# The second MLP layer of a diffusion block on one core: one more level of the seven-product scheme

## The chip, the cores and the metric

The kernel runs on one core of a Trainium2 chip. A core has a matrix engine (TensorE, PE in the profile) that reads SBUF and writes PSUM, a vector engine (VectorE, DVE), a scalar engine (ScalarE, ACT), a general engine (GpSimd, POOL) and a queue engine that starts transfers (SyncE, SP). Each takes its instructions in the order of the program; semaphores order the engines among each other. The metric is the device time of one launch in microseconds, median of 3 runs: 2862.96 (2862.67 to 2863.17).

## The reference

One layer is computed for 256 context tokens and 2048 latent tokens of width 1024: modulated norm, input projection, attention and Fourier mixing, output projection with a gated residual, and then an MLP with a squared ReLU. The part that matters here is the last:

```
def sq_relu_mlp(h, w1, w2):
    return jnp.square(jax.nn.relu(h @ w1)) @ w2
...
        xs = xs + g2 * sq_relu_mlp(h, w1[l], w2[l])
```

The second product has 2304 tokens (18 tiles of 128), an inner width of 4096 and 1024 output columns. All of it is in 32-bit floats.

## The kernel before

**Precision.** Every operand of a large product is split into a high part, which ScalarE makes by a copy to the type F32R, and a low part, which VectorE makes by subtracting the high part from the operand (two inputs in SBUF). `mm3` (line 93) then issues three matmuls for one product of tiles: high x high, high x low, low x high. TensorE reads F32R in one pass.

**Seven products.** The MLP's second layer is cut in two along tokens (9 tiles each), inner width (16 tiles of 128 each) and output columns (512 each), and the four block products per quadrant are replaced by the seven products of Strassen's scheme in Winograd's form. `PO` (line 1383) is their order: 1, 2, 6, 7, 5, 3, 4. The sums of token blocks are made in the first layer by GpSimd (`g_add`, line 1784) and stored to DRAM (`sop`, tile `sd`); the sums of weight blocks were made earlier too (`tsum`); product 4 subtracts two of its raw weight tiles at the time of use.

**The second layer's loop** (from line 2020) runs over the 7 products `i`, over 3 blocks `b` of 3 token tiles, and over 16 inner tiles `k`. For each `k` it issues 3 x 3 matmuls: the stationary operand is a token tile (128 x 128), the moving one is a weight tile of 512 columns. Three PSUM banks collect a block; six are in use in turn. `t_prep` (line 1401) splits one weight tile of 512 columns, 16 per product; `s_prep` (line 1415) splits token operands in pieces of 768 columns, 24 per product. `t_load` and `s_load` bring the raw operands in by SP's queue some steps ahead. When a block is done, `y_post` (line 1973) combines its three banks with the running sums `UU` and `U3` in SBUF, and, in the products 2, 5, 3 and 4, which finish outputs, multiplies by the gate, adds the residual and lets `y_store` store it. GpSimd has no instruction in this loop. The split operands live in rings: `op` (9 pairs of 512 columns, shared with the first layer) and a second ring of 13.

The order of the work is the order of the Python calls, written out by hand (`tc.manual_schedule()`): each engine runs its own instructions in that order, as soon as the semaphores allow.

Of the kernel before, what the change touches and what calls it, by code (L numbers as in the profile page):

```python
# [37 lines left out]
def f32(ap):  # L38
    return ap.bitcast(F32)


def body(tc, a, out):
    nc = tc.nc
    ctx = ExitStack()
    with ctx:
# [1336 lines left out]
        OPB, AHEAD = 9, 6  # L1382
        PO = (1, 2, 6, 7, 5, 3, 4)
        w2s = a["w2"][0].rearrange("(n k p) o -> p n k o", p=P, k=16)
        TR, TO, SR, SO, own = {}, {}, {}, {}, {}

        def op(nm, shared=True):
            if shared:
                return [ms2.tile([P, 512], F32R, tag=f"op{x}", name=f"op{x}{nm}", bufs=OPB) for x in "hl"]
            return [own["wk"].tile([P, 512], F32R, tag=f"t{x}", name=f"t{x}{nm}", bufs=16 + AHEAD - OPB) for x in "hl"]  # L1390

        def t_load(n):

            p, k = PO[n // 16], n % 16
            TR[n] = []
            for rc in {1: (11,), 2: (21,), 3: (22,), 5: (0,), 7: (1,), 6: (2,), 4: (2, 21)}[p]:
                r, c = divmod(rc, 10)
                src = w2s[:, r - 1, k, (c - 1) * 512:c * 512] if r else tsum[k][:, c]
                TR[n].append(raw(f"b{rc}_{n}", src))

        def t_prep(n):
            src, *more = TR.pop(n)
            for t in more:
                nc.vector.tensor_sub(src, src, t)
            hi, lo = op(f"T{n}", n % (16 + AHEAD) < OPB)
            nc.scalar.copy(hi, src)
            nc.vector.tensor_sub(lo, src, f32(hi))
            TO[n] = hi, lo

        def s_load(m):  # L1410
            i, r = divmod(m, 12)
            b, c = divmod(r, 4)
            SR[m] = hr_load(f"sr{m}", sop[PO[i]][b][:, 4 * c:4 * c + 4, :])

        def s_prep(m):
            src = SR[m // 2][:, m % 2 * 2:m % 2 * 2 + 2, :]
            pool, bufs = (ms2s, 2) if m % 3 < 2 else (own["t6"], 1)
            hi, lo = (pool.tile([P, 2, 384], F32R, tag=f"s{x}", name=f"s{x}{m}", bufs=bufs) for x in "hl")
            nc.scalar.copy(hi, src)  # L1419
            nc.vector.tensor_sub(lo, src, f32(hi))  # L1420
            SO[m] = hi, lo

# [280 lines left out]
        with c5r, ExitStack() as c5:  # L1706
# [157 lines left out]
            with tc.manual_schedule():  # L1864
                for n, (q, p) in enumerate(ITEMS):
# [70 lines left out]
                    if q == NQ - 1 and p == 7:  # L1936
                        s_load(0)
                        for n in range(4):
                            t_load(n)
                        s_load(1)  # L1940
# [191 lines left out]
```

## Time and profile before

| what | us |
|---|---|
| median of 3 runs | 2862.96 |
| the profiled execution, first to last instruction | 2861.4 |
| stage 0 to 530 (conditioning, projections), TensorE busy | 516.31 |
| stage 530 to 1245 (attention), TensorE busy | 707.81 |
| stage 1245 to 1470 (output projection), TensorE busy | 223.17 |
| stage 1470 to 2170 (MLP, first layer), TensorE busy | 698.45 |
| stage 2170 to 2857 (MLP, second layer), TensorE busy | 685.91 |

The profile was taken on one execution; its span lies 1.6 us below the median of the runs. How to read its lines: a group of instructions is named by line, engine and operation, output tile <- input tiles, shapes and count, then busy time, mean duration in ns, and the idle time of the engine before them with what ended it. A line of a timeline has start and duration in us. A line of the windows has, for a stretch, the busy time and number of instructions of PE, PEld (weight loads), DVE, ACT and POOL, then the granted clock of TensorE, the share of the transfer engines and GB/s. In the second layer the weight tiles of the split operands are called `thT`, `tlT`, `ophT`, `oplT`, and the token pieces `sh` and `sl`.

### The profile page before, as it was taken

The page shows a single profiled execution, that of the slowest core. Times are in us where ns is not written, and L with a number is a line of the kernel's source. Part 1 is how long each engine was busy: PE and PEld are TensorE (multiplying, and loading weights), DVE is VectorE, ACT ScalarE, POOL GpSimd, SP SyncE. Part 2 cuts the span into 40 slices and gives each one's busy share as a digit, 9 for nine tenths or more (in the row PEclk, how much of TensorE's full clock was granted, in tenths as well). Part 3 has the DMA queues.
Part 4 walks back from the last instruction along what each step waited for, and adds up shares of the span by engine and source line. Part 5 has one row for each costly group of instructions (what it writes and reads, how often), then busy time and mean ns, then how long its engine had stood idle before and what let it go on. Part 6 is the DMA issues. An engine that isn't in the chain of part 4 may idle for free.

```text
span 2861.4 us, 43224 instructions
## 1 busy us (share of the span) xinstructions
PE 2831.7 (99%) x15109; PEld 2455.9 (86%) x15109; DVE 2018.0 (71%) x3393; ACT 1548.2 (54%) x3505; POOL 1073.3 (38%) x890
## 2 busy tenths in 40 slices
PE   8999999999999999999999999999999999999999
PEld 5888888688888888888889999999998888888887
DVE  7767886898988989864477777778775354345554
ACT  4333323798989989853356565556555332333221
POOL 1211223798999989942223333333332000000000
PEclk9999999999999999999999999999999999999999
DMA  7776777421211212036767676667747464445663
GB/s 284 219 207 198 230 213 237 172 106 38 73 71 53 106 38 99 23 124 201 242 221 232 223 246 228 221 219 238 234 167 255 147 202 135 138 144 185 206 206 111
DMA packets 392780, 492.94 MB, mean 172 GB/s; under 512 B 26467, under 2 KB 306384, under 8 KB 389490
## 3 DMA queue, kind: packets, MB, share of 16 engines
q1 hardware_dynamic: 387136, 479.73, 50.9%
q0 software_dynamic: 1872, 7.28, 0.8%
q10 hardware_dynamic: 3554, 3.17, 0.4%
q8 instruction: 119, 1.95, 0.3%
q14 instruction: 99, 0.81, 0.1%
HBM read 312.58 MB, written 179.59 MB: 172 GB/s over the span
## 4 chain that ended last, share of the span: by engine, by line
PE 54%; DVE 1%; DMA 0%; ACT 0%; issue 0%; SPq 0%; POOL 0%; DVEq 0%; POOLq 0%
PE ps L94 8%; PE ps L95 8%; PE ps L96 8%; PE pB L1749 2%; PE pB L1747 2%; PE pB L1748 2%; PE pA L1748 2%; PE pC L1748 2%; PE pA L1749 2%; PE pC L1747 2%; PE pA L1747 2%; PE pC L1749 2%; PE po L94 2%; PE po L96 2%; PE po L95 2%; PE pD L1749 1%
## 5 line engine op out<-in xcount | busy, mean ns | idle before, releaser
L1085 DVE TENSOR_REDUCE mxs<-Ss 128x1 f32<-128x512 f32 x636 | 405.4, 686 | 65.5 <-PE Ss L1080 55.1
L1420 DVE TENSOR_TENSOR sl<-sr,sh 128x768 fp32r<-128x768 f32 x168 | 161.8, 964 | 331.5 <-ACT sh L1419 331.1
L1120 POOL TENSOR_TENSOR P0s<-P0s,P1s 128x1024 f32<-128x1024 f32 (+2 forms) x128 | 378.6, 2958 | 10.7
L1419 ACT CAST sh<-sr 128x768 fp32r<-128x768 f32 x168 | 140.6, 838 | 418.3 <-PE ps L95 418.3
L1789 POOL TENSOR_TENSOR gs<-g,g 128x384 f32<-128x384 f32 x48 | 69.7, 1452 | 468.5 <-ACT g L1759 418.9
L1104 ACT ACTIVATE P1s<-Ss,mxs 128x512 f32<-128x512 f32 x318 | 215.4, 694 | 36.3 <-DVE mxs L1088 35.3
L94 PE MATMUL pj<-wh,hh 128*128 128x512 f32 x576 | 228.8, 397 | 2.0 <-DVE hh L555 2.0
L94 PE MATMUL ps<-thT,sh 128*128 128x512 f32 x585 | 227.6, 389 | 0.0
L95 PE MATMUL ps<-tlT,sh 128*128 128x512 f32 x585 | 227.6, 389 | 0.0
L96 PE MATMUL ps<-thT,sl 128*128 128x512 f32 x585 | 227.6, 389 | 0.0
L95 PE MATMUL pj<-wl,hh 128*128 128x512 f32 x576 | 227.1, 394 | 0.5 <-DVE wl L516 0.5
L96 PE MATMUL pj<-wh,hl 128*128 128x512 f32 x576 | 225.6, 392 | 0.0
L1104 ACT ACTIVATE P0s<-Ss,mxs 128x512 f32<-128x512 f32 x318 | 214.3, 691 | 5.6 <-DVE mxs L1088 5.0
L1135 PE MATMUL pts<-ident,P0s 128*128 128x128 f32 x1280 | 191.7, 273 | 4.5 <-DVE als L1147 1.8
L1080 PE MATMUL Ss<-KS0s,Qs 128*128 128x512 f32 x636 | 190.1, 419 | 0.4 <-ACT P1s L1104 0.4
L1080 PE MATMUL Ss<-KS1s,Qs 128*128 128x512 f32 x636 | 188.7, 420 | 1.5 <-ACT P0s L1104 1.4
L1758 ACT ACTIVATE g<-uz 128x384 f32<-128x384 f32 x144 | 75.7, 526 | 200.2 <-DVE uz L1781 174.1
L1135 PEld LDWEIGHTS pts<-ident,P0s 128*128 128x128 f32 x1280 | 151.3, 140 | 35.9 <-issue 4.8
L1119 POOL TENSOR_SCALAR P1s<-P1s,tots 128x1024 f32<-128x1024 f32 (+2 forms) x128 | 171.9, 1343 | 5.8
L1147 DVE TENSOR_TENSOR als<-pts,ahs 128x512 fp32r<-128x512 f32 x256 | 165.9, 681 | 6.9 <-ACT ahs L1142 6.7
L94 PE MATMUL ps<-ophT,sh 128*128 128x512 f32 x423 | 164.7, 389 | 1.1 <-DVE uz L1781 1.1
L96 PE MATMUL ps<-ophT,sl 128*128 128x512 f32 x423 | 164.6, 389 | 0.0
(536 smaller groups left out, 8073.9 us busy)
## 6 DMA issues: line engine op xcount, KB each, us to landing
sr<-sd SPq DMA_DIRECT2D x84, 768.0 KB, 4.5
a<-in_w SPq DMA_DIRECT2D x184, 256.0 KB, 4.2
sd<-gs SPq DMA_DIRECT2D x192, 192.0 KB, 1.9
sd<-g SPq DMA_DIRECT2D x144, 192.0 KB, 2.1
wm<-in_w_mod SPq DMA_DIRECT2D x32, 512.0 KB, 5.2
Qs<-qd SPq DMA_DIRECT2D x32, 512.0 KB, 4.0
b<-in_w SPq DMA_DIRECT2D x64, 256.0 KB, 5.8
b<-tsum SPq DMA_DIRECT2D x64, 256.0 KB, 4.7
```

The costliest lines, as they stand in the source:

```text
L94: nc.tensor.matmul(ps, lh, rh, start=first, stop=False)
L95: nc.tensor.matmul(ps, lh, rl, start=False, stop=False)
L96: nc.tensor.matmul(ps, ll, rh, start=False, stop=last)
L1080: nc.tensor.matmul(S[:, :w], self.Q[:, x, m, j * P:j * P + P], self.hd.KS[m][:, b * 512:b * 512 + w], start=(x == 0), stop=(x == 1))
L1085: nc.vector.tensor_reduce(self.mx[j][:, m, b:b + 1], self.S[j, m, b], axis=AX.X, op=ALU.max)
L1104: nc.scalar.activation(dst, S, AF.Exp, bias=self.mx[j][:, m, 6:7], accum_out=self.sm[j][:, m, b:b + 1])
L1119: nc.gpsimd.tensor_scalar(p, p, tot[:, 3:4], 0.0, op0=ALU.mult, op1=ALU.add)
L1120: nc.gpsimd.tensor_add(d, d, p)
L1135: nc.tensor.transpose(pt[:, c:c + P], self.p0[j][:, (kb + t) * P:(kb + t + 1) * P], ident)
L1747: nc.tensor.matmul(ps, wh[:, c], hh[:, k, :], start=first and k == 0, stop=False, skip_group_check=True)
L1748: nc.tensor.matmul(ps, wh[:, c], hl[:, k, :], start=False, stop=False, skip_group_check=True)
L1749: nc.tensor.matmul(ps, wl[:, c], hh[:, k, :], start=False, stop=k == 3, skip_group_check=True)
```

## The change

Each of the seven products, until now a plain product of (9 token tiles) x (16 inner tiles) x 512 columns, is itself done by the same seven-product scheme: 8 of the token tiles are cut in two halves of 4, the inner tiles in two halves of 8, and the columns in two halves of 256. The ninth token tile ("o") is done plainly, with 512 columns. A product is now 56 units `u`: 7 parts `s` of 8 inner tiles `k`. A unit issues 4 x 3 matmuls of 256 columns, and in the parts 0 and 2 another 3 of 512 columns for the ninth tile. The 4 tiles of a part share one PSUM tile of 1024 columns (two banks); three of these and two of one bank are in use in turn.

The sums of operands that the inner scheme needs are made in SBUF, in place, by GpSimd: `y_sum` on weight tiles, 256 columns each, 4 x 8 per product; `x_sum` on token rows, 3 x 4 of 1024 columns and 8 of 512 per product. Afterwards `prep` splits the operands for each unit as before (ScalarE copy, VectorE subtraction), 3 units ahead. The results are put together by `s_copy` and `t7_copy` (ScalarE), `u3_make` (VectorE and GpSimd), `pre` (GpSimd, 1024 columns) and `fin` (VectorE, one input in PSUM). `gain` and `resid` are VectorE's multiplication by the gate and addition of the residual, 1024 columns each.

Weight tiles wait in `ya` (8 tiles, tag `raw`) and `yb` (8), token rows in `hr` and `x3`, `x20`, `x21` and a ring of 5 (`x12`); most are loaded again for the next product once their last use in this one is over. The half row that `x12` holds is loaded twice per product. `do(u, ...)` files a task under the unit at which it is issued; tasks of rank under 2 come ahead of that unit's `prep`, the others behind it.

The core of the diff (`-` lines of the loop that it replaces, described above, are left out):

```diff
@@ -1379,49 +1379,114 @@
-        OPB, AHEAD = 9, 6
+        OPB = 9
...
+        UPS, LSP = 56, 3
+        TA, TB, B1, B2, B4, X12, PT, PS_ = {}, {}, {}, {}, {}, {}, {}, {}
...
+        def t_load(i, k):
+            src, *more = t_src(i, k)
+            if k < 8:
+                t = TA[i, k] = raw(f"ya{i}_{k}", src)
+            else:
+                t = TB[i, k - 8] = own["wk"].tile([P, 512], F32, tag="yb", name=f"yb{i}_{k}", bufs=8)
+                nc.sync.dma_start(t, src)
+            for m in more:
+                d = own["wk"].tile([P, 512], F32, tag="yt", name=f"yt{i}_{k}", bufs=2)
+                nc.sync.dma_start(d, m)
+                nc.vector.tensor_sub(t, t, d)
...
+        def x2_load(i, m, h):
+            t = own["t6"].tile([P, 2, 512], F32, tag=f"x2{h}", name=f"x2{h}_{i}_{m}", bufs=4)
+            s_cols(t, i, 8 * h + 2 * m, 2, 1)
+            (B4 if h else B2)[i, m] = t
+        def x12_load(i, k, first):
+            n = X12.setdefault("n", 0)
+            X12["n"] = n + 1
...
+            s_cols(t[:, 0:512].unsqueeze(1), i, 8 + k, 1, 0)
+            if first:
+                nc.sync.dma_start(t[:, 512:640], sop[PO[i]][2][:, 8 + k, 256:384])
+            X12[i, k] = t
+        def split(nm, src):
+            hi, lo = op(nm)
+            for n, x in enumerate(src):
+                c = slice(n * x.shape[1], (n + 1) * x.shape[1])
+                nc.scalar.copy(hi[:, c], x)
+                nc.vector.tensor_sub(lo[:, c], x, f32(hi[:, c]))
+            return hi, lo
+        def y_part(i, s, k):
+            t, c = {1: (TA, 1), 3: (TA, 1), 4: (TA, 0), 5: (TB, 0), 6: (TB, 1)}[s]
+            return t[i, k][:, c * 256:c * 256 + 256]
+        def prep(u):
+            i, r = divmod(u, UPS)
+            s, k = divmod(r, 8)
+            nm = f"{i}_{s}_{k}"
+            if s in (0, 2):
+                t = split("t" + nm, [(TB if s else TA)[i, k]])
+            elif k % 2 == 0:
+                hi, lo = split("t" + nm, [y_part(i, s, k + n) for n in range(2)])
+                t = hi[:, 0:256], lo[:, 0:256]
+                PT[u + 1] = hi[:, 256:512], lo[:, 256:512]
+            else:
+                t = PT.pop(u)
...
@@ -1957,113 +2024,229 @@
...
+            def pre(i, x):
+                p, f = PO[i], L2[i, "3"] if x[0] == "2" else L2[i, "2"]
+                d = DST[i, x] = temp(i, x)
                 if p == 1:
                     return
+                if p == 4:
+                    nc.gpsimd.tensor_sub(d, d, f)
+                    return
+                nc.gpsimd.tensor_add(d, U3[x] if p == 5 else UU[x], f)
+                if p == 5:
+                    nc.gpsimd.tensor_add(UU[x], UU[x], f)
+            def fin(i, x, ps):
+                p = PO[i]
+                v = ps if x == "o" else ps.rearrange("p (t c) -> p t c", t=4)
+                minus = (x == "21") != (p == 4)
+                if x in ("11", "o"):
+                    d = DST[i, x] = temp(i, x)
+                    if p == 1:
+                        nc.scalar.copy(d, v)
+                        return
+                    src = {2: UU, 6: UU, 7: UU, 5: U3, 3: UU, 4: U3}[p][x]
+                else:
+                    d = DST[i, x]
+                    src = d if p != 1 else L2[i, "3"] if x[0] == "2" else L2[i, "2"]
+                (nc.vector.tensor_sub if minus else nc.vector.tensor_add)(*((d, src, v) if minus else (d, v, src)))
+                if p == 5:
+                    (nc.vector.tensor_sub if minus else nc.vector.tensor_add)(*((UU[x], UU[x], v) if minus else (UU[x], v, UU[x])))
+            def gain(i, x):
+                d = DST[i, x]
+                for t0, n, s, _, c in places(i, x)[0]:
+                    if x == "o":
+                        nc.vector.tensor_mul(d, d, g2[s][:, c])
+                    else:
+                        v = d[:, t0:t0 + n, :]
+                        nc.vector.tensor_mul(v, v, g2[s][:, c].unsqueeze(1).to_broadcast([P, n, 256]))
+            def resid(i, x):
+                nc.vector.tensor_add(DST[i, x], DST[i, x], X[x])
...
+            def u3_make(i):
+                t, d = L2[i, "s"], L2[i, "7"]
+                nc.vector.tensor_add(flat2(t), BANK[i, "B"], flat2(t))
+                nc.gpsimd.tensor_sub(d, t, d)
+                L2[i, "3"], L2[i, "2"] = t, d
+            def y_sum(n, i, k):
+                a, b = TA[i, k], TB[i, k]
+                d1, d3, d2, d4 = a[:, 0:256], a[:, 256:512], b[:, 0:256], b[:, 256:512]
+                if n == 3:
+                    nc.gpsimd.tensor_sub(d3, d4, d3)
+                elif n == 2:
+                    nc.gpsimd.tensor_add(d3, d3, d1)
+                elif n == 1:
+                    nc.gpsimd.tensor_sub(d1, d4, d3)
+                else:
+                    nc.gpsimd.tensor_sub(d2, d3, d2)
+            def x_sum(n, i, m):
+                if n == 4:
+                    d = row(B2, i, m)
+                    nc.gpsimd.tensor_sub(d, X12.pop((i, m))[:, 0:512], d)
+                    return
+                b1, b2 = B1[i, m][0], B2[i, m]
+                if n == 3:
+                    nc.gpsimd.tensor_sub(b2, b1, b2)
+                elif n == 2:
+                    nc.gpsimd.tensor_sub(b2, B4[i, m], b2)
+                else:
+                    nc.gpsimd.tensor_add(b1, b2, b1)
...
+            BK = "ABABCDC"
             for i in range(7):
+                u0 = i * UPS
+                p = PO[i]
+                for k in range(8):
+                    if i:
+                        do(u0 + k - 8, 0, t_load, i, k)
+                    do(u0 + k - 5, 0, t_load, i, k + 8)
+                    do(u0 + 9 + k, 0, x12_load, i, k, True)
+                    do(u0 + 37 + k, 0, x12_load, i, k, False)
+                    for n, u in ((3, 1), (2, 10), (1, 18), (4, 27)):
+                        do(u0 + u + k, 1, y_sum, n, i, k)
+                    do(u0 + 41 + k, 1, x_sum, 4, i, k)
+                for m in range(4):
+                    if i or m > 2:
+                        do(u0 + 2 * m - 8, 0, x11_load, i, m)
+                    do(u0 + 2 * m - 4, 0, x2_load, i, m, 0)
+                    do(u0 + 2 * m + 4, 0, x2_load, i, m, 1)
+                    for n, u in ((3, 1), (2, 10), (1, 18)):
+                        do(u0 + u + 2 * m, 1, x_sum, n, i, m)
+                do(u0 + 9, 3, s_copy, i)
+                do(u0 + 17, 3, t7_copy, i)
+                do(u0 + 34, 3, u3_make, i)
+                for x, b, e in (("11", "A", 26), ("o", "o", 32), ("22", "C", 42), ("21", "D", 50), ("12", "C", 58)):
+                    if x in NB[1:]:
+                        do(u0 + e - (6 if i == 6 and x == "12" else 3), 1.5, pre, i, x)
+                    if i == 6 and x == "12":
+                        continue
+                    do(u0 + e, 3, lambda i, x, b: fin(i, x, BANK[i, b]), i, x, b)
+                    if p in (2, 5, 3, 4):
+                        do(u0 + e - 3, 0, x_load, i, x)
+                        do(u0 + e + 1, 3, gain, i, x)
+                        do(u0 + e + 2, 3, resid, i, x)
+                        do(u0 + e + (3 if x == "o" else 4), 0, y_store, i, x)
...
+            def bank(i, s):
+                if s in (0, 1, 4, 5):
+                    BANK[i, BK[s]] = pp.tile([P, 1024], F32, tag="ps", name=f"ps{i}_{s}", bufs=3)
+                if s == 0:
+                    BANK[i, "o"] = pp.tile([P, 512], F32, tag="po", name=f"po{i}", bufs=2)
+                return BANK[i, BK[s]], BANK[i, "o"]
+            def mm3s(ps, l, r, first, last):
+                for n, (x, y) in enumerate(((0, 0), (0, 1), (1, 0))):
+                    nc.tensor.matmul(ps, l[x], r[y], start=first and not n, stop=last and n == 2, skip_group_check=True)
...
+                hold = []
+                for u in range(7 * UPS):
+                    i, r = divmod(u, UPS)
+                    s, k = divmod(r, 8)
+                    tasks = sorted(TASK.pop(u, ()), key=lambda e: e[:3])
+                    for e in tasks:
+                        if e[0] < 2:
+                            e[3](*e[4])
+                    if LSP <= u + LSP < 7 * UPS:
+                        prep(u + LSP)
+                    for e in tasks:
+                        if e[0] > 2:
+                            e[3](*e[4])
+                    if k == 0:
+                        ps, po = bank(i, s)
+                    hold.append((k, PT.pop(("u", u))))
+                    if u >= 7 * UPS - 3 and u < 7 * UPS - 1:
+                        continue
+                    for j in range(4):
+                        c = slice(j * P, j * P + P)
+                        for kk, (t, sx) in hold:
+                            mm3s(ps[:, j * 256:j * 256 + 256], (sx[0][:, c], sx[1][:, c]), (t[0][:, 0:256], t[1][:, 0:256]),
+                                 s in (0, 1, 4, 5) and kk == 0 and j % 2 == 0, kk == 7 and s not in (0, 1, 4))
+                    for kk, (t, sx) in hold:
+                        if s in (0, 2):
+                            mm3s(po, sx[2:4], t, s == 0 and kk == 0, s == 2 and kk == 7)
+                    hold.clear()
+                d, z = DST[6, "12"], L2[6, "s"]
+                c = places(6, "12")[2]
+                for j in range(4):
+                    nc.vector.tensor_mul(z[:, j, :], ps[:, j * 256:j * 256 + 256], g2[0][:, c])
+                    nc.vector.tensor_sub(d[:, j, :], d[:, j, :], z[:, j, :])
+                    r = (NTH + j) * P - NP
+                    nc.sync.dma_start(out[1][0][r:r + P, c], d[:, j, :])
```

More of the change, by code (lines that the diff above doesn't have):

```diff
@@ L1392, in t_load @@
[L1392 to L1396, printed above, removed]
-                r, c = divmod(rc, 10)
[L1398 to L1421, printed above, removed]
+        own = {}
@@ new lines, in row @@
+        def row(B, i, k):
+            return B[i, k // 2][:, k % 2, :]
+        def split(nm, src):
[8 more added lines that the diff above has]
+            return t[i, k][:, c * 256:c * 256 + 256]
```

213 lines of the change are left out of this document (108 added, 105 removed).

## The prediction

> **What bounds the kernel now.** I read the page's totals first, then the windows of the stage that changes, then its tiles, its waits, and the timelines of the other engines for prices.
>
> ```profile
> span 2861.4 us, 43224 instructions
> core 0: us, PE busy (x) PEld busy (x) DVE busy (x) ACT busy (x) POOL busy (x), PEclk, DMA share, GB/s
> 2169.00:2857.00 688.00, 686.91 (x3031) 568.31 (x3029) 329.32 (x433) 205.19 (x291) 5.75 (x4) 1.00 0.51 171
> ```
> ```profile
> L94 PE MATMUL ps<-thT,sh x585: 389/389/389, 2189.8 to 2854.8; 128*128 128x512 f32 x195
> L94 PE MATMUL ps<-ophT,sh x423: 389/389/496, 2170.0 to 2856.2; 128*128 128x512 f32 x141
> L96 PE MATMUL ps<-ophT,sl x423: 388/389/397, 2170.5 to 2856.6; 128*128 128x512 f32 x141
> ```
> ```profile
> ACT sh L1419 <- PE ps L95: 418.3, 148, 3.3
> DVE sl L1420 <- ACT sh L1419: 331.1, 138, 3.1
> ```
> The second layer is the last quarter of the span, and PE is its bound: busy without a hole, full clock, while ACT waits 418 us for PE to give operand buffers back and DVE waits behind ACT. GpSimd (POOL) has 4 instructions there. PE runs 3 x (585 + 423) = 3024 matmuls of 512 columns from 2170.0 to 2856.7, 686.7 us: one each 0.227 us. The 389 ns of a row are pipelined latency, not cost.
>
> **The change, part by part.** *TensorE.* A product now has 7 x 8 x 4 x 3 = 672 matmuls of 256 columns and, for the ninth token tile, 16 x 3 = 48 of 512. The attention stage shows the price of 256 columns with the same three-term form and a new weight load each time:
>
> ```profile
> 804.34 0.28 PE L95 MATMUL po<-als,Vs 128*128 128x256 f32 x1
> ...
> 805.48 0.28 PE L96 MATMUL po<-ahs,Vs 128*128 128x256 f32 x1
> ```
> Eleven starts, ten intervals, take 1.14 us, so 0.114 us each: half of 0.227, with the weight loads hidden. One product: 672 x 0.114 + 48 x 0.227 = 87.5 us; seven: 612.5. TensorE gives up **74 us**.
>
> *VectorE.* Each operand is split in two: ACT copies the high part, DVE subtracts for the low one. A product had 16 splits of 512 and 24 of 768 columns; it gets 56 + 16 of 512, 40 of 256 and 16 of 128. Prices:
>
> ```profile
> 1804.60 0.69 DVE L1451 TENSOR_TENSOR oplW<-ws,ophW 128x512 fp32r<-128x512 f32 x1
> 1805.20 0.69 DVE L1719 TENSOR_TENSOR ws<-a,ws 128x512 f32<-128x512 f32 x1
> ```
> ```profile
> L349 DVE TENSOR_TENSOR qt<-qn,tb 128x256 f32<-128x256 f32 x64 | 24.1, 419 | 0.0
> L340 DVE TENSOR_TENSOR tb<-rp,kg 128x128 f32<-128x128 f32 x16 | 4.6, 287 | 0.0
> L1577 DVE TENSOR_TENSOR ml<-mT,mh 128x1024 fp32r<-128x1024 f32 x17 | 20.8, 1226 | 0.7
> L1406 ACT CAST thT<-b 128x512 fp32r<-128x512 f32 x65 | 39.5, 617 | 41.1 <-DVE b L1404 31.2 <-PE ps L96 8.5 <-DMA b<-tsum 1.4
> ```
> Back to back, 0.69 us costs 0.60; taking the same 0.09 off the others gives 0.33 (256), 0.20 (128) and 1.14 (1024). Splits: 72 x 0.60 + 40 x 0.33 + 16 x 0.20 = 59.6 us per product. Four products also write outputs, with 8 gains and residual adds of 1024 and 2 of 512: 10.3 us each; product 4 subtracts 16 raw pairs: 9.6. Over seven: 417 + 41 + 10 = **468 us** of instructions that read two SBUF operands. The combinations that read PSUM (4 of 1024, one of 512, one more 1024 addition per product) come beside these. ACT has 128 copies of at most 0.617 us, 79 us per product: under TensorE's 87.5, so free.
>
> *GpSimd.* New per product: 32 sums of 256 columns (weights), 8 of 512 and 12 of 1024 (tokens), one 1024 for the recombination; three more of 1024 (`pre`) in all but product 1, six in product 5. Prices, alone:
>
> ```profile
> L1226 POOL TENSOR_TENSOR P0p<-P0p,P1p 128x256 f32<-128x256 f32 x8 | 5.9, 739 | 0.7
> L1120 POOL TENSOR_TENSOR P0s<-P0s,P1s 128x512 f32<-128x512 f32 x1 | 1.3, 1282 | 0.1
> L1120 POOL TENSOR_TENSOR P0s<-P0s,P1s 128x1024 f32<-128x1024 f32 x63 | 151.4, 2403 | 5.3
> ```
> ```profile
> 1508.86 1.02 POOL L1791 TENSOR_TENSOR gs<-gs,g 128x384 f32<-128x384 f32 x1
> 1509.84 1.47 POOL L1793 TENSOR_TENSOR gs<-g,g 128x384 f32<-128x384 f32 x1
> ```
> An interval is 0.04 us under the duration: 0.70, 1.24, 2.36. So 32 x 0.70 + 8 x 1.24 + 13 x 2.36 = 63 us per product, 441 in all, and 21 x 2.36 = 50 for `pre`: **491 us**, 392 instructions. By itself that fits under 612.
>
> *The two together* do not:
>
> ```profile
> L1793 POOL TENSOR_TENSOR gs<-g,g x48: 1014/1243/2547, 1497.5 to 2175.8; 128x384 f32<-128x384 f32 x48
> L1451 DVE TENSOR_TENSOR oplW<-a,ophW x140: 680/682/1522, 1464.0 to 2158.3; 128x512 fp32r<-128x512 f32 x140
> L1781 DVE TENSOR_TENSOR uz<-pC,u x96: 547/558/558, 1482.1 to 2171.3; 128x384 f32<-128x384 f32 x96
> ```
> ```profile
> 2173.09 1.02 POOL L1789 TENSOR_TENSOR gs<-g,g 128x384 f32<-128x384 f32 x1 [7.48 <-ACT g L1759]
> 2174.18 1.61 POOL L1791 TENSOR_TENSOR gs<-gs,g 128x384 f32<-128x384 f32 x1
> 2175.76 1.74 POOL L1793 TENSOR_TENSOR gs<-g,g 128x384 f32<-128x384 f32 x1
> 2177.46 1.46 POOL L1795 TENSOR_TENSOR gs<-g,gs 128x384 f32<-128x384 f32 x1
> ```
> ```profile
> 2173.77 2.84 DVE L1420 TENSOR_TENSOR sl<-sr,sh 128x768 fp32r<-128x768 f32 x2 [1.28 <-ACT sh L1419]
> 2176.54 2.93 DVE L1407 TENSOR_TENSOR oplT<-b,ophT 128x512 fp32r<-128x512 f32 x2
> ```
> A two-operand SBUF subtraction on DVE reaches 1.52 us where 0.68 is its own: 0.84 more, a whole GpSimd instruction. GpSimd in turn reaches 2.55 for 1.01. DVE's form with a PSUM operand (L1781) never exceeds 0.56. In the last two fences the very splits of this layer meet four GpSimd sums: they take strict turns, 2173.09 to 2179.47, 6.38 us. Their intervals alone would be 4 x 0.98 + 2 x 0.86 + 2 x 0.60 = 6.84. So the two engines share one resource, a turn costs about its own time, and 0.12 us is saved per GpSimd instruction.
>
> The Trainium skill says the same ("SBUF — State Buffer", section "Who interferes with whom"): a VectorE instruction with two SBUF inputs and a GpSimd instruction that reads SBUF exclude each other, and the second to issue blocks until the first ends. The four turns above agree (0.84 us over); that it holds for 1024 columns no run here shows.
>
> **The sum.** Shared resource: 468 + 491 - 392 x 0.12 = 912 us for a stage in which TensorE needs 612. Waits in which neither engine uses it are not in the rows of before. At least 0: GpSimd's queue may always hold ready work. At most 7 us per product, if all of DVE's PSUM-reading instructions (about six at the 1.14 of 1024 columns) find GpSimd with nothing to do. I take 2, nearer to 0 since GpSimd is seldom done: 14 us. Stage 926, against 686.7: +239. On the profiled 2861.4 that is 3100.7; the median of the runs, 2862.96, is 1.6 more: **3102**, rounded to 3100.
>
> Where it will wait: GpSimd's queue is in order. The `u3_make` subtraction sits behind TensorE's fourth part, the next product's first sums behind a reload of `yb` and `x20`. Behind them stand all later sums, and behind those DVE's splits, its `fin` (for `pre`) and TensorE.
>
> ```profile
> sr<-sd SPq DMA_DIRECT2D x84, 768.0 KB, 4.5
> b<-tsum SPq DMA_DIRECT2D x64, 256.0 KB, 4.7
> L1376 SPq DMA_DIRECT2D sr<-sd x84: 319/320/510, 2155.7 to 2822.0; - x84
> ```
> Those reloads land in some 4.7 us, while DVE splits for part 0. SP issues some 106 transfers per product (16 + 12 + 16 + 40 for operands, 17 + 5 for residuals and stores), 34 to 54 us at 0.32 to 0.51; and 8 x 256 KB come on top of 16 x 256 + 12 x 768, since half an operand row is loaded twice. Both are hidden in 130 us.
>
> **The rivals.**
> (a) *TensorE stays the bound* (faster). If DVE and GpSimd met as rarely as in the first layer, the stage would take 612: 2861.4 - 74 + 1.6 = 2789. For it: each engine alone fits (468 and 491 under 612). Against it: together they need 912, and nothing can keep them apart. Its place is the whole stage, its price the 74 us; it decides once the shared time is under 612.
>
> (b) *Partial exclusion.*
> ```profile
> L1789 POOL TENSOR_TENSOR gs<-g,g 128x384 f32<-128x384 f32 x48 | 69.7, 1452 | 468.5 <-ACT g L1759 418.9 <-DVE ws L1719 32.4 <-DMA b<-in_w 9.6
> L1791 POOL TENSOR_TENSOR gs<-gs,g 128x384 f32<-128x384 f32 x48 | 53.0, 1104 | 3.7
> ```
> These are the costliest and the cheapest of the first layer's four sums; their middle, 1278 ns, is 1.26 times the least, 1014. GpSimd at 491 x 1.26 = 619 would just bound the stage: 2795. With a 0.55 us turn before each of its 392 instructions it has 491 + 216 = 707: 2883. This takes DVE's other splits as free, which the turns speak against.
>
> (c) *TensorE's pauses halve its clock*, on top of the forecast.
> ```profile
> 32.62 0.79 PE L94 MATMUL pj<-wh,hh 128*128 128x512 f32 x1 [1.98 <-DVE hh L555]
> 30.00:40.00 10.00, 8.02 (x28) 6.40 (x28) 9.48 (x22) 9.60 (x21) 0.93 (x1) 0.66 0.88 331
> ```
> Around a pause of 1.98 us, with light work before it, TensorE was granted 0.66 of its clock over 10 us, a loss of 3.4. Four such pauses per product are 28 x 3.4 = 95 us: 3197; eight are 190: 3292. For it: TensorE will be idle a third of the stage. Against: the idle comes in pieces of about 1 us per unit, and while TensorE is not the bound, a slow spell costs nothing. The Trainium skill ("TensorE: Matmul & The Clock Gate", Part 1) halves the clock after an idle window of about 3.4 us. The row agrees that idle time costs clock, and shows it after a shorter pause.
>
> (d) *It doesn't do what it says*: a compiler that put the sums on DVE would make DVE the bound, with its times under the forecast's and no turns; the code names the engine of each sum, so I give this nothing of its own.
>
> **How the numbers follow.** Forecast 0.75, with its own range 3024 to 3184. Low: pure column times without any gap between instructions, POOL (2403 - 1282)/512 = 2.19 ns, DVE (1226 - 690)/512 = 1.05 ns a column: with the counts above, 200,704 columns x 2.19 + 389,120 x 1.05 = 848 us, so 3024. High: no saving at the turns and 7 us of waits per product, 959 + 49 = 1008, so 3184. Rival (c) 0.12, 3197 to 3292; (a) 0.05, 2789; (b) 0.08, 2795 to 2883, which is half faster and half slower. The range 3015 to 3205 holds the forecast's 0.75 and about a third of (c), its milder cases: 0.79. Faster by over 0.2% (about what a measurement of this kernel can tell from no change): 0.05 + 0.03 = 0.08; within: 0.01; slower: 0.91.
>
> **What would show it.** Right: in the stage, DVE's 512-column subtractions far above 0.69 us and GpSimd's sums above their own times; DVE and GpSimd both near fully busy; TensorE busy about two thirds, waiting for DVE's low parts; the ACT wait for PE's buffers nearly gone; 256-column intervals of 0.114 where TensorE is fed. Wrong: TensorE without holes and a stage near 612 (a); GpSimd full while DVE's instructions keep their own times (b); a granted clock clearly under 1 in the stage (c). If both engines show long idle times together, the 2 us of waits are the term that failed, and the time lies above the range.

## The result, and the profile after

The changed kernel takes **3140.66 us** (median of 4 runs, 3139.37 to 3143.35), against 2863.07 for the kernel before in the same series: 1.097 times as long, with a 95% interval of 1.096 to 1.099. The profiled execution has a span of 3139.7 us. The forecast was 3100 with a range of 3015 to 3205. Before the change the second layer took 687 us and the rest of the kernel 2176; the rest is unchanged, and the second layer now takes 3140.7 - 2176 = 965 us. In the same way "the stage" of every kernel below is its median less 2176.

The page's totals, and the windows of the stage (columns as before: PE, PEld, DVE, ACT, POOL, then granted clock, DMA share, GB/s):

```profile
span 3139.7 us, 50317 instructions
PE 2902.6 (92%) x17125; PEld 2588.3 (82%) x17125; DVE 2601.3 (83%) x3967; ACT 1774.4 (57%) x4128; POOL 1714.5 (55%) x1282
...
2169.00:3140.00 971.00, 758.09 (x5049) 700.22 (x5047) 914.86 (x1010) 433.29 (x915) 646.53 (x396) 0.89 0.43 138
```

TensorE was busy in 687 of 688 us before; now it stands idle for 213 of 971, and its mean clock is 0.89. VectorE is the full engine: 915 us busy, 56 idle. An engine counts as busy while one of its instructions stands in line for something it shares. Some of its groups and GpSimd's in that stretch, with busy time, mean ns of one, and the idle time ahead of them:

```profile
L1452 DVE TENSOR_TENSOR opls<-x,ophs 128x512 fp32r<-128x512 f32 x392 | 426.8, 1113 | 10.1 <-ACT ophs L1451 10.1
L1487 DVE TENSOR_TENSOR odl<-x,odh 128x128 fp32r<-128x128 f32 x112 | 83.1, 742 | 3.9 <-POOL gs L1860 3.9
L2156 POOL TENSOR_TENSOR x<-x,x 128x1024 f32<-128x1024 f32 x28 | 78.7, 2810 | 0.0
L2137 POOL TENSOR_TENSOR ya<-yb,ya 128x256 f32<-128x256 f32 x56 | 70.4, 1265 | 120.0 <-DVE oplt L1452 79.3 <-DMA x<-sd 31.1 <-DVE odl L1487 9.6
L2130 POOL TENSOR_TENSOR t<-s,t 128x1024 f32<-128x1024 f32 x7 | 41.2, 5882 | 127.6 <-DVE s L2129 127.6
L2129 DVE TENSOR_TENSOR s<-ps,s 128x1024 f32<-128x1024 f32 x7 | 8.5, 1211 | 0.0
```
```profile
L1452 DVE TENSOR_TENSOR opls<-x,ophs x392: 673/681/2897, 2169.6 to 3126.8; 128x512 fp32r<-128x512 f32 x196
```

The last line gives minimum, median and maximum of the 392 low parts: more than half of them run at their own 0.68 us, and the rest wait, up to 2.9 us. A mean of 1113 ns is not a slower engine but a mixture of two cases. The 128-column ones, 0.29 us by themselves, show 0.74. The addition that reads PSUM (L2129) keeps its own time. In GpSimd's column the recombination (L2130) takes 5.9 us where 1024 columns alone take 2.4. How the two engines meet, in the timelines of VectorE and, below the gap, GpSimd (start, duration):

```profile
2477.77 2.87 DVE L1452 TENSOR_TENSOR opls<-x,ophs 128x512 fp32r<-128x512 f32 x1
2480.56 0.82 DVE L1487 TENSOR_TENSOR odl<-x,odh 128x128 fp32r<-128x128 f32 x1
2481.30 1.22 DVE L1452 TENSOR_TENSOR oplt<-yb,opht 128x512 fp32r<-128x512 f32 x1
2482.45 2.85 DVE L1452 TENSOR_TENSOR opls<-x,ophs 128x512 fp32r<-128x512 f32 x1
...
2477.38 2.71 POOL L2154 TENSOR_TENSOR x<-x,x 128x1024 f32<-128x1024 f32 x1 [0.68 <-POOL ya L2139]
2480.05 1.18 POOL L2139 TENSOR_TENSOR ya<-ya 128x256 f32<-128x256 f32 x1
2481.19 0.79 POOL L2141 TENSOR_TENSOR ya<-yb,ya 128x256 f32<-128x256 f32 x1
2481.94 2.80 POOL L2156 TENSOR_TENSOR x<-x,x 128x1024 f32<-128x1024 f32 x1
```

VectorE's first split is issued at 2477.77, 0.39 us into a GpSimd sum of 1024 columns, and ends at 2480.64, 0.55 after that sum: nearly all of its own 0.68 comes behind it. Then each waits for the other in turn, three instructions of each in 4.7 us. Waits of the stage (total, times, longest):

```profile
ACT ophs L1451 <- PE ps L2213: 256.5, 180, 7.9
...
PE ps L2213 <- DVE opls L1452: 157.0, 110, 4.9
ACT opht L1451 <- PE ps L2213: 139.4, 77, 9.0
POOL t L2130 <- DVE s L2129: 127.6, 7, 21.6
POOL ya L2137 <- DVE oplt L1452: 79.3, 23, 23.8
...
PE ps L2213 <- DVE oplt L1452: 39.7, 26, 5.5
```

TensorE waits 197 us for low parts. ScalarE still waits 396 us "for PE": it runs ahead until the ring of split operands is full, and TensorE gives them back late because the low parts come late. This line has the same form as in the kernel before, where TensorE was the bound; only the next step along the chain tells the two apart.

### The profile page after: what moved, and what is told of

Same layout as the page of the kernel before. It is cut to its first block, busy times and chain, and to the rows that moved or that the text cites. A ratio compares the mean times of both kernels' runs of the same rounds, so it can differ in the third digit from the quotient of the medians.

```text
span 3139.7 us, 50317 instructions
## 1 busy us (share of the span) xinstructions
PE 2902.6 (92%) x17125; PEld 2588.3 (82%) x17125; DVE 2601.3 (83%) x3967; ACT 1774.4 (57%) x4128; POOL 1714.5 (55%) x1282
## 4 chain that ended last, share of the span: by engine, by line
PE 36%; DVE 14%; DMA 4%; issue 4%; SPq 1%; POOL 1%; ACT 0%; DVEq 0%; ACTq 0%; POOLq 0%
PE ps L2213 8%; DVE opls L1452 7%; DVE oplt L1452 4%; DMA x<-sd 2%; PE pB L1813 2%; PE pB L1814 2%; PE pB L1812 2%; PE pA L1813 2%; PE pC L1814 2%; PE pC L1813 2%; PE pC L1812 2%; PE pA L1814 2%; PE pA L1812 2%; PE po L94 2%; PE po L96 2%
## 5 line engine op out<-in xcount | busy, mean ns | idle before, releaser
L2213 PE MATMUL ps<-opht,opls 128*128 128x256 f32 x1568 | 485.7, 310 | 158.1 <-DVE opls L1452 157.0
L2213 PE MATMUL ps<-oplt,ophs 128*128 128x256 f32 x1568 | 472.3, 301 | 39.8 <-DVE oplt L1452 39.7
L2213 PEld LDWEIGHTS ps<-opht,opls 128*128 128x128 f32 x1568 | 324.6, 207 | 188.0 <-DVE opls L1452 187.1
L2213 PE MATMUL ps<-opht,ophs 128*128 128x256 f32 x1568 | 467.8, 298 | 4.0 <-ACT ophs L1451 4.0
L1452 DVE TENSOR_TENSOR opls<-x,ophs 128x512 fp32r<-128x512 f32 x392 | 426.8, 1113 | 10.1 <-ACT ophs L1451 10.1
L1451 ACT CAST ophs<-x 128x512 fp32r<-128x512 f32 x392 | 233.3, 618 | 319.4 <-PE ps L2213 256.5
L2213 PEld LDWEIGHTS ps<-oplt,ophs 128*128 128x128 f32 x1568 | 325.1, 207 | 53.9 <-DVE oplt L1452 49.0
L2213 PEld LDWEIGHTS ps<-opht,ophs 128*128 128x128 f32 x1568 | 326.7, 208 | 10.9 <-ACT ophs L1451 4.7
L303 POOL TENSOR_TENSOR qrs<-qss,mhalf 128x8 f32<-128x8 f32 x36 | 69.5, 1934 | 246.3 <-DVE qss L302 246.2
L1452 DVE TENSOR_TENSOR oplt<-ya,opht 128x256 fp32r<-128x256 f32 (+1 forms) x224 | 188.5, 870 | 1.9 <-ACT opht L1451 1.7
```

Of the source, the lines that this page charges most:

```text
L1451: nc.scalar.copy(hi[:, c], x)
L1452: nc.vector.tensor_sub(lo[:, c], x, f32(hi[:, c]))
L2213: nc.tensor.matmul(ps, l[x], r[y], start=first and not n, stop=last and n == 2, skip_group_check=True)
```

## The experiments

Theory: **the shared resource of VectorE and GpSimd** ("the port" below) is the bound. Rivals: clock lost in TensorE's pauses, GpSimd's queue order, and the loads that the change repeats. Each kernel is the changed one with one edit, unless two are named. Behind each time stands its ratio to the kernel before, with the 95% interval.

### Taking the port away

**e2_low_psum.** The ninth tile's split is edited in the same way, and its PSUM ring cut to one tile to make room.

```diff
-                nc.vector.tensor_sub(lo[:, c], x, f32(hi[:, c]))
+                nc.vector.tensor_sub(lo[:, c], x, own["zp"][:, c] if "zp" in own else f32(hi[:, c]))
...
+            own["zp"] = pp.tile([P, 512], F32, tag="zp", name="zp", bufs=1)
+            for j in range(4):
+                nc.tensor.transpose(own["zp"][:, j * P:j * P + P], ident, ident)
```

> Every low part of the second layer (from unit 3 on) is the operand minus a constant tile in PSUM instead of minus the high part in SBUF, so the low parts are not the real ones; counts, shapes and the order on every engine stay as they are, GpSimd's sums too. Port theory (DVE's two-input SBUF form and GpSimd's sums exclude each other): only gains, residuals and product 4's subtractions still share, so the stage falls from 967 to 640 to 740 us, the whole to 2815 to 2915, and the 512-column subtractions are back near 0.68 us each, GpSimd's 1024-column sums near 2.4. Queue theory (GpSimd's own slowness and its waits in order set the pace): the stage stays above 880, the whole above 3055. Clock theory (TensorE's pauses): nothing changes, 3120 to 3150.

Measured: 2883.95 us, 1.007 (1.005 to 1.009), in the port theory's range; the stage 708, 257 less than in the changed kernel. Windows, groups:

```profile
2169.00:2882.00 713.00, 667.53 (x5058) 642.71 (x5056) 567.61 (x1010) 428.48 (x916) 511.36 (x396) 0.97 0.58 188
```
```profile
L1452 DVE TENSOR_TENSOR opls<-x,zp 128x512 fp32r<-128x512 f32 x389 | 256.1, 682 | 73.1 <-PE ps L2216 57.6 <-DMA x<-sd 14.0
...
L2159 POOL TENSOR_TENSOR x<-x,x 128x1024 f32<-128x1024 f32 x28 | 67.7, 2418 | 0.0
```

The same number of instructions of the same sizes on the same engines; what is changed is where one input lies. The low parts are at 682 ns instead of 1113, GpSimd's sums at 2418 instead of 2810, and both engines have time to spare. One thing more goes with the edit: a low part no longer waits for ScalarE's copy. In the changed kernel that wait was 12 us in all (10.1 and 1.7), too little for 257, and the next run keeps it. The two together show the port as the cause.

**e8_memset.** The other side of it: GpSimd stays busy, but reads nothing.

```diff
+            def gset(d, *_):
+                for _ in range(2):
+                    nc.gpsimd.memset(d, 0.0)
...
-                    nc.gpsimd.tensor_sub(d3, d4, d3)
+                    gset(d3, d4, d3)                        # and so for all sums
```

> Each operand sum on GpSimd is replaced by two memsets of the same destination, which read nothing; the sums are left out. GpSimd stays busy for a similar time per sum and writes the same tiles, so it still waits for the same last readers. Port theory: no reads on GpSimd's side, the stage falls to 620 to 720 us, the whole to 2795 to 2895, with DVE's 512-column subtractions near 0.68. If writes share as reads do, the stage stays near 900 and the whole near 3080. Queue theory: above 3055 as well.

Measured: 2891.40 us, 1.010 (1.008 to 1.012), again as the port theory has it; the stage 715. Windows and groups:

```profile
2169.00:2891.00 722.00, 671.89 (x5070) 645.99 (x5068) 592.57 (x1011) 430.89 (x918) 420.02 (x761) 0.97 0.58 187
```
```profile
L1452 DVE TENSOR_TENSOR opls<-x,ophs 128x512 fp32r<-128x512 f32 x392 | 273.5, 716 | 71.3 <-ACT ophs L1451 68.1 <-DMA x<-sd 0.7
L2135 POOL MEMSET x<- 128x1024 f32 x168 | 160.4, 955 | 32.9 <-DMA x<-sd 25.2 <-DVE opls L1452 2.8
```

GpSimd is still busy for 420 us, in the same places of its queue, and still waits for the last readers of the tiles that it writes (106 us for low parts, where the changed kernel has 79); VectorE's two-SBUF subtractions are nearly at their own time. So it is GpSimd's *reading*, not its being busy or writing, that holds VectorE. The Trainium skill ("SBUF — State Buffer", section "Who interferes with whom") says just this: a VectorE instruction with two SBUF inputs contends with a GpSimd instruction that reads SBUF, not with one that only writes it. The two runs agree with it, 682 and 716 ns against 1113.

**e4_pe_less** and **e5_u3_dve** test two rivals, TensorE's clock and GpSimd's queue.

```diff
                    for j in range(4):
+                        if j > 1 and k not in (0, 7):
+                            continue
```
```diff
-                nc.gpsimd.tensor_sub(d, t, d)               # in u3_make
+                nc.vector.tensor_sub(d, t, d)
```

> For two of the four token tiles only the first and last inner tile of each part are multiplied: TensorE's 256-column matmuls fall by 37.5 per cent (612 to about 410 us at full clock), everything else stays. Port theory: TensorE was waiting anyway, 3110 to 3141. Clock theory: TensorE's time counts, so the time falls by 60 us or more, under 3080.

Measured: 3131.28 us, 1.094 (1.092 to 1.095).

```profile
2169.00:3140.00 971.00, 636.93 (x3310) 548.33 (x3308) 898.11 (x1011) 426.79 (x918) 680.83 (x396) 0.76 0.43 138
```

A third of the stage's matmuls are gone, TensorE's busy time falls by 121 us, its clock to 0.76, and the kernel is 9 us faster. So a third less work for TensorE, at a still lower clock, is worth 9 us while the port is the bound. The clock theory, which asked for 60 or more, falls.

> The subtraction of u3_make (1024 columns, once per product) goes from GpSimd to DVE, right behind the addition it waits for, so GpSimd's queue no longer stands still 128 us in all there. Port theory: while GpSimd waits, DVE has the port to itself, so that wait costs nothing; 7 x (2.36 - 1.14) = 9 us less at most, 3125 to 3145. Queue theory: most of 128 us comes back, under 3050.

Measured: 3141.52 us, 1.097 (1.095 to 1.099), no change. VectorE is busy or in line for 922 us of the same window, as before for 915. By itself this run doesn't decide against the queue theory, because most of the wait only moved: the next instructions of GpSimd's queue, those of `pre`, read the same addition's result, and now stand where the subtraction stood.

```profile
POOL uu L2077 <- DVE s L2129: 35.4, 2, 19.2
POOL u L2077 <- DVE s L2129: 35.4, 2, 19.2
...
POOL u L2075 <- DVE s L2129: 19.1, 1, 19.1
```

That is 90 of the 128 us. What speaks against the queue theory is e2, where GpSimd's queue holds the same instructions in the same order and 257 us go all the same, and e7 below, where there is no such queue and the time is 2964, not the 2884 that this theory gives.

### Moving the sums to VectorE

If the port is one queue, GpSimd's instruction of 2.4 us per 1024 columns is the dear one in it: VectorE does the same sum in 1.2. So moving *more* work to the fullest engine should make the kernel faster.

```diff
-                    nc.gpsimd.tensor_sub(d3, d4, d3)        # e3: y_sum and x_sum; e6: x_sum only;
+                    nc.vector.tensor_sub(d3, d4, d3)        # e7: these, u3_make and pre
```

> All operand sums, u3_make's subtraction and pre go to DVE; GpSimd has nothing left in the second layer. Port theory: DVE's own two-input work is 468 us plus 7 x (32 x 0.33 + 8 x 0.60 + 12 x 1.14) = 203 for the sums, 28 x 1.14 = 32 for u3_make and pre, and 49 for the instructions that read PSUM: 752. DVE alone sets the stage, 750 to 790 us, the whole 2926 to 2966, every 512-column subtraction at 0.68, and faster than the change as it stands although DVE has more to do. Queue theory: with no GpSimd queue to wait for, the stage is as in the run with the low parts from PSUM, about 707, the whole 2884.

Measured: 2964.08 us, 1.035 (1.032 to 1.038), in the port theory's range.

```profile
2169.00:2962.00 793.00, 707.87 (x5047) 655.25 (x5045) 761.42 (x1401) 432.81 (x913) 4.80 (x4) 0.96 0.52 169
```

> The token sums (x_sum) go to DVE, the weight sums (y_sum), u3_make and pre stay on GpSimd: a dose between. Port theory: DVE 468 + 7 x (8 x 0.60 + 12 x 1.14) = 129 + 49 = 646, GpSimd's turns 7 x 32 x 0.70 + 66 = 223 less 252 x 0.12 = 30: 839, so a stage of 810 to 860 and a whole of 2986 to 3036. If the number of GpSimd's turns counts and not their length, three fifths of the 260 us stay: about 3040.

Measured: 3031.76 us, 1.059 (1.056 to 1.062), in its range too: fewer sums moved, less gained. It is no test of turns against their length: the rival's "about 3040" lies only 8 us away.

> Only the operand sums (y_sum, x_sum) go to DVE; u3_make's subtraction and pre stay on GpSimd, 28 instructions of 2.36 us. Port theory: DVE 468 + 203 + 49 = 720, and up to 66 of GpSimd's turns on top: stage 735 to 790, whole 2911 to 2966, not better than with those on DVE as well. Queue theory: about 2884.

Measured: 2987.49 us, 1.043 (1.040 to 1.046), 21 us above the upper end of what the port theory gave; but its order held: e3 with 28 instructions left on GpSimd is slower than e7 with none. Those 28 cost the 23 us between the two kernels and the 32 us of VectorE's time (28 x 1.14) that moving them adds, 55 us or 1.97 each, no more than the 2.36 of a 1024-column sum. So the turns are not what was priced too low. VectorE stands idle for 70 us of e3's window, which the forecast left out; 36 of them it waits for `pre` on GpSimd. How GpSimd's subtraction in `u3_make` fares:

```profile
L2130 POOL TENSOR_TENSOR t<-s,t 128x1024 f32<-128x1024 f32 x7 | 78.1, 11159 | 617.7 <-DVE s L2129 617.7
```

11.2 us for a sum of 2.4: with VectorE always in line, GpSimd's turn comes late, and `pre`, for which VectorE waits, comes behind it.

So with 364 sums and 28 recombinations moved onto the fullest engine, the kernel is 177 us faster than the changed one. It still is slower than the kernel before, since VectorE then needs 761 us.

**e1_no_sums** leaves the sums out everywhere.

```diff
             def y_sum(n, i, k):
+                return
```

> The operand sums are left out on every engine. What remains on DVE is 468 + 49, on GpSimd 66: 583 us, under TensorE's 643 (672 x 0.120 + 48 x 0.235 per product, by the intervals of the run with the low parts from PSUM). Port theory: TensorE is the bound, stage 645 to 700, whole 2821 to 2876: the floor of this way of cutting the product, and hardly under the kernel before. If DMA or the order of loads set the pace in that run, it stays near 707 and 2884.

Measured: 2902.64 us, 1.014 (1.011 to 1.017), above the expected range, and the stage at 726 even above e2's 708. The expectation had TensorE at 0.120 us a matmul already, which the next section works out. So by these prices neither TensorE nor the port alone explains e1's stage, and something else adds to it. Why e1 lies above e2 was not taken apart; one difference is that VectorE waits 93 us for ScalarE's copies in e1, which e2's low parts don't need.

### What is left without the port

In e2, where TensorE runs without a hole for stretches, its timeline shows this (20 intervals from the first line to the last):

```profile
2450.00 0.28 PE L2216 MATMUL ps<-opht,ophs 128*128 128x256 f32 x1
...
2452.40 0.28 PE L2216 MATMUL ps<-opht,opls 128*128 128x256 f32 x1
```

2.40 / 20 = 0.120 us, not 0.114. The kernel before had a row with the same message, three intervals of 384 columns:

```profile
1496.05 0.34 PE L1749 MATMUL pD<-mhh,oplW 128*128 128x384 f32 x1
...
1496.57 0.34 PE L1749 MATMUL pD<-mhh,oplW 128*128 128x384 f32 x1
```

0.52 / 3 = 0.173. Intervals of 0.227, 0.173 and 0.120 for 512, 384 and 256 columns lie on a line with 13 ns at no columns: halving the columns does not halve the interval. The ninth token tile's 512 columns show 0.235 between the others (2481.99, 2482.22, 2482.46 in the changed kernel). TensorE's need in the stage is 4704 x 0.120 + 336 x 0.235 = **643** us, and the change saves it 44, not 74.

That leaves e2's stage 65 us over TensorE. e9 joins e2 and e4, to see what is under TensorE.

> Both edits at once: low parts from the PSUM constant (not the real low parts), and for two of the four token tiles only the first and last inner tile of each part multiplied. It asks what holds the 708 us of the run with the low parts from PSUM. If TensorE does (its intervals there are 0.120 us, 643 us in all, not the 612 of the forecast): TensorE's work falls to 7 x (420 x 0.120 + 48 x 0.235) = 432 us, and DVE, busy 568 us there, is next: stage 580 to 650, whole 2756 to 2826. If loads, reloads and the order of the queues hold it: stage 690 to 710, whole 2866 to 2886.

Measured: 2842.78 us, 0.993 (0.991 to 0.995), between the two expectations; the stage 667.

```profile
2169.00:2844.00 675.00, 510.39 (x3309) 462.63 (x3307) 584.61 (x1010) 405.93 (x917) 507.81 (x396) 0.88 0.61 198
```

No engine is full: 510, 585, 406 and 508 of 675 us. What remains is a transfer or an order. So the loads that are repeated for each product were left out, in the changed kernel (e10), in e2 (e11) and in e9 (e12):

```diff
         def x2_load(i, m, h):
+            if i:                                            # t_load and x11_load likewise
+                D = B4 if h else B2
+                D[i, m] = D[0, m]
+                return
```

> The changed kernel, but the second layer's products 2 to 7 use the operand tiles of product 1 again: the loads of ya, yb, x11, x20 and x21 and product 4's subtractions of a second weight tile are left out (x12, residuals and stores stay), so only product 1 is computed from its own operands. Theory of the shared port: DVE loses 8 subtractions (12 us with their blocking) and little else, since GpSimd waits for transfers only 31 + 5 us by the rows of the changed kernel; 3095 to 3135. Rival, the reloads set the waits of the stage (GpSimd's first sums behind a reload, all later ones behind them): DVE's 56 us without work go as well, 3050 to 3095.

> As e2_low_psum (low parts from a constant PSUM tile), with the same reloads left out. In e2_low_psum the stage takes 708 us where TensorE's intervals (4704 of 0.120, 336 of 0.235) add up to 643. Theory: those 65 us are waits for reloads; then the stage comes to 643 to 670, the kernel to 2820 to 2848. Rival: they are GpSimd sums that still hold DVE's gains and the operands, and clock lost after pauses; then no more than 15 us go, 2868 to 2884.

> As e9_low_psum_pe_less (low parts from a constant PSUM tile, and two of four token tiles only at k 0 and 7), with the same reloads left out. e9's stage took 667 us with TensorE at 510, VectorE at 585, GpSimd at 508 and bursts of transfers. Theory: the bunched reloads are its floor; the stage falls to VectorE's busy time and a little, 575 to 620, the kernel to 2752 to 2797. Rival: the floor is the order of the instructions of VectorE, ScalarE and GpSimd among each other; the stage stays at 645 to 667, the kernel at 2822 to 2843.

Measured: e10 3117.36 us, 1.089 (1.088 to 1.091); e11 2841.31 us, 0.993 (0.991 to 0.994); e12 2772.82 us, 0.969 (0.967 to 0.970). Their windows, in this order:

```profile
2169.00:3117.00 948.00, 757.41 (x5049) 704.09 (x5047) 904.52 (x994) 434.43 (x915) 664.55 (x396) 0.89 0.22 67
```
```profile
2169.00:2840.00 671.00, 648.60 (x5053) 631.93 (x5051) 554.05 (x994) 429.58 (x915) 512.16 (x396) 0.99 0.31 94
```
```profile
2169.00:2772.00 603.00, 489.68 (x3295) 455.53 (x3293) 569.02 (x992) 406.70 (x912) 509.40 (x396) 0.89 0.34 104
```

Beside the port the loads matter little: e10 is 23 us faster than the changed kernel, 10 of them less busy time of VectorE, which has product 4's 16 subtractions less, and 13 less idle time (43 against 56). Without the port they are the next cost: e11's stage is 665 against e2's 708, its TensorE busy for 649 of 671 us at a clock of 0.99, close to its 643. e12's falls by 70 us to VectorE's busy time and a little. So each floor was found under the one before: the port (257 us), then the loads with the waits for them (43), then TensorE at 643.

The loads are hardly too many: e2's transfers take 0.58 of the transfer engines' time. They come in bunches, as its transfer row over 40 slices of the stage shows (busy tenths, 9 is 90% or more):

```profile
DMA  7960697215899219931099301699702799572262
```

Slices of 9 stand beside slices of 0 to 2, since a product's operands are all loaded in the few units between their last use and their next. That the bunching, and not the number of loads, costs the 43 us is not shown: a spread-out order was not tried.

## Why the prediction was right, and where it was wrong

The forecast had the right mechanism, and the time lies inside its own range (3024 to 3184), 41 us above its middle. Two of its terms were off.

**TensorE.** "TensorE gives up 74 us" was wrong: 44. The 0.114 came from eleven starts in the attention stage; the row of 384 columns in the same trace would have corrected it. While TensorE isn't the bound, this changes nothing in the sum (e4: 121 us less of its time gives 9), but it changes rival (a).

**VectorE's and GpSimd's own times** (468 and 491 us) held: e2 and e7 show the low parts at 682 ns and at a median of 705, and e2's sums at 2418. In all, VectorE is busy for 761 us in e7, where the prices add up to 752, and GpSimd for 511 in e2, where they add up to 491.

**"The two together do not" fit** was right, and is shown by e2, e8 and the three kernels that move sums. It carries nearly the whole result: 257 of the 278 us that the change costs go when the inputs are moved to PSUM. It holds for sums of 1024 columns too, which the rows of before could not show (the 2.87 us at 2477.77). One reading was loose: the 0.84 us that the slowest subtraction of the first layer lost is less than the 0.98 of a whole GpSimd sum, and it stands in the row of L1451, not in the four turns.

**The mis-sized term is the waits in which neither engine uses the port.** 468 + 491 - 47 = 912 of the stage's 965 are the shared time; 53 us remain, where the forecast took 14, from a range of 0 to 49. These 39 us are the whole distance between 3102 and 3141. The trace bears the split out: laid over each other, VectorE's instructions with two SBUF inputs and GpSimd's cover 910 of the window's 971 us. The reason for a low value was that "GpSimd is seldom done". It has 971 - 647 = 324 us without work. It waits 128 us for the addition in `u3_make` and 79 for low parts: `y_sum` 3 writes `ya` in place, so it must wait until part 0 has split that tile; the forecast had named only the reload there. So VectorE's PSUM-reading instructions (seven per product, 51 us in all) mostly found GpSimd without work: for 41 of the 51 us. And for 25 us of the window, 3 of them its end, neither engine works at all, which even the upper end of 7 us per product left out; with it the sum would have given 3137. (Instructions that follow each other overlap a little, so 41 and 25 are more than the 61 us beside the 910.) Of VectorE's 56 us without work, 21 are waits for `pre`, while GpSimd works, 13 for the transfers of product 4's second weight tiles, and 12 for ScalarE's copies. e10 puts 13 on the reloads, which the forecast had called hidden.

**What would show it.** Right: low parts far above 0.69 us, GpSimd's sums above their own times, TensorE waiting for low parts. Half right: "DVE and GpSimd both near fully busy" holds for VectorE (94%), not for GpSimd (67%); "TensorE busy about two thirds" came out as 78% (758 of 971). "Both engines show long idle times together" was named as the sign that the 2 us had failed; together they are idle for 25 us only, and the larger part of the 53 is VectorE reading PSUM while GpSimd has no work. Wrong: "the ACT wait for PE's buffers nearly gone" (396 us), since any late step behind ScalarE fills its ring; "256-column intervals of 0.114".

**The rivals.** (a), 2789, was wrong in its price too: with no port, e2 gives 2884, and with no reloads either, e11 gives 2841. (b), VectorE's instructions at their own times beside a full GpSimd, falls by the maximum of 2897 ns. (c): the clock did fall, to 0.89, and e4 gives no sign that it costs more than 9 us, as the forecast's own counter-argument said: while TensorE isn't the bound, a slow spell costs next to nothing. The three kernels here that are faster than the one before (e9, e11, e12) leave work out.

## What to carry to other kernels

Before work is moved to an idle engine, ask what it shares with the busy one: two engines with 468 and 491 us of work did not fit under TensorE's 643, because they read through one port, and moving the work *back* to the fuller engine gained 177 us. Price a shorter instruction from a long unbroken run of its kind, at two sizes, so that the fixed part shows; a burst flatters. And a saving on the bounding engine is worth no more than the distance to the next floor: TensorE gives up 44 us, and even with the port and the loads both taken away, 21 of them were left.

## What the runs showed of the hardware

- After a pause TensorE's rate can be halved, though not after each. The changed kernel's timeline, with the waits in brackets:

```profile
2485.35 0.58 PE L2213 MATMUL ps<-opht,opls 128*128 128x256 f32 x1 [2.27 <-DVE opls L1452]
2485.73 0.42 PE L2213 MATMUL ps<-opht,ophs 128*128 128x256 f32 x1
2485.95 0.42 PE L2213 MATMUL ps<-oplt,ophs 128*128 128x256 f32 x1
2486.16 0.41 PE L2213 MATMUL ps<-opht,opls 128*128 128x256 f32 x1
...
2494.67 0.38 PE L2213 MATMUL ps<-opht,opls 128*128 128x256 f32 x1 [2.27 <-DVE opls L1452]
2494.89 0.28 PE L2213 MATMUL ps<-opht,ophs 128*128 128x256 f32 x1
2495.01 0.28 PE L2213 MATMUL ps<-oplt,ophs 128*128 128x256 f32 x1
```

  The first four show intervals of 0.21 to 0.22 from the second on, after 2.27 us without work, where 0.12 is usual. Behind another pause of 2.27 us they are 0.12 from the second on, and 0.21 only from 2495.62. So the length of the pause alone doesn't tell. The Trainium skill ("TensorE: Matmul & The Clock Gate", Part 1) names about 3.4 us of idle time for such a halving; both pauses here were shorter.

- The port does not always change hands after each instruction. In e2 the gains are among VectorE's few instructions that still need it, and one of them stood in line for 11 us while GpSimd ended one sum and did twelve more. The gains of one tile (minimum, median, maximum), then VectorE's timeline and GpSimd's:

```profile
L2109 DVE TENSOR_TENSOR uu<-uu,g x6: 679/1394/11030, 2697.5 to 2789.2; 128x512 f32<-128x512 f32 x4, 128x1024 f32<-128x1024 f32 x2
```
```profile
2697.51 11.63 DVE L2109 TENSOR_TENSOR uu<-uu,g 128x512 f32<-128x512 f32 x2
...
2698.02 1.42 POOL L2144 TENSOR_TENSOR ya<-yb,ya 128x256 f32<-128x256 f32 x2
2699.41 2.40 POOL L2159 TENSOR_TENSOR x<-x,x 128x1024 f32<-128x1024 f32 x1
2701.78 0.73 POOL L2144 TENSOR_TENSOR ya<-yb,ya 128x256 f32<-128x256 f32 x1
2702.48 5.51 POOL L2146 TENSOR_TENSOR yb<-ya,yb 128x256 f32<-128x256 f32 x8
```

  By itself a gain takes 0.68. GpSimd's sums keep their own times all through, and VectorE comes in only when they are over, at 2708. In e3 it is the other way round: each of the seven subtractions of `u3_make` stands in line while some 17 instructions of VectorE keep their own times, and has its 2.4 us only when VectorE has run out of ready instructions that need the port. Why the turns are strict in the changed kernel and not in these two stays open.
